# A scheduling priority around two groups of stages in a one-layer trunk kernel

## The chip, the core and the metric

The kernel runs on one core of a Trainium2 chip. The core has five engines with a queue each: PE (TensorE, matmuls), DVE (VectorE), ACT (ScalarE), POOL (GpSimd) and SP (SyncE, which here issues DMAs only). Each engine takes its instructions in the order of the program and waits at one whose inputs are not there. The metric is the device time of one execution in microseconds; times of kernels are medians of several runs.

## What is computed

One layer over 512 tokens with 1024 features, all in float32:

```python
h = rms_norm(x, g_mix)
p = h @ w_in
y_a = mla_group(p[..., :MLA_COLS], ...)     # 8 heads of latent attention, block-causal
y_b = rwkv7_group(p[..., MLA_COLS:], ...)   # 8 heads of a delta-rule recurrence over the tokens
x = x + concat(y_a, y_b) @ w_o
x = x + peer_ffn(rms_norm(x, g_ffn), ...)   # below
...
q = (hb @ w_pq).reshape(TOK_BLOCK, PEER_HEADS, 2, PEER_DHALF)
s = einsum('thpd,hpnd->thpn', q, sub_keys)
s1, i1 = top_k(s[:, :, 0], 16); s2, i2 = top_k(s[:, :, 1], 16)
top_s, pos = top_k(s1[..., :, None] + s2[..., None, :], 16)     # of 256 sums
idx = take_along_axis(i1 * 128 + i2, pos)                       # 16 of 16384 experts, per head
act = gelu(einsum('thkd,td->thk', expert_u[idx], hb))
out = einsum('thk,thkd->td', softmax(top_s) * act, expert_v[idx])
```

Each of the 16384 experts has one row of 1024 numbers in `expert_u` and one in `expert_v`, 64 MB each.

## The kernel before

The tokens are four blocks of 128. Every block runs through five stages, each a Python generator: F (`front`: norm and the projection for the recurrence), R (`chunks`: the recurrence's chunk-local products, with an inverse of triangular systems that alternates PE, line 674, and DVE, line 683), M (`latent`: the attention), S (`scan`: the recurrence over chunks) and B (`back`: output projection, line 792; retrieval, whose queries are line 848 on PE and whose top-16 lists are lines 827 to 835 on DVE; and routing, which ends on PE in line 947 and then writes the indices `idx` on ACT, line 960). I write F0 for stage F of block 0 and so on; blocks 1 and 2 share one B stage, B12. Block 0 and block 3 each have a B of their own, B0 and B3, the latter being the last entry of the list `BACK`.

Then the experts are worked off in two ways. Blocks 1 and 2 are dense: `dense()` goes through all experts in 128 tiles, with `up(e)` (line 1103 or 1117 on PE), `gate_half` (lines 1035 to 1043) and `down(e)` (line 1134 on DVE, then 1138 or 1149 on PE). Blocks 0 and 3 gather: `experts(b)` fetches, for each of 128 places (8 heads x 16), one row of `expert_u` per token by an indirect DMA that POOL issues (line 978), multiplies and sums it on DVE (line 988), and later does the same with `expert_v` (line 991). That makes 256 gathered tiles of 512 KB per block, 512 in all, in a ring of four buffers `ga`. One gather row below means one of these tiles and its DVE instruction.

A loop emits the steps of the stages in an order worked out from rough costs (`at`), `dense()` and the two `experts` behind them all. This is not yet the order on the engines. A scheduler goes over all the emitted instructions and fills each engine's queue with whatever it holds to be ready, by the priority of an instruction, lowest number first. The priority is a counter that rises by one with each instruction that is emitted. Waits are added where an instruction needs another engine's result or a buffer that is still in use. All loads of weights and tokens go through SP's queue in its order.

Of the kernel before, what the change touches and what calls it, by code (L numbers as in the profile page):

```python
# [29 lines left out]
TOPK = 16  # L30
# [5 lines left out]
# columns of the packed per-channel vectors  # L36
# [7 lines left out]
# columns of the packed per-feature rows  # L44
# [6 lines left out]
# candidate pairs (a, b) of the two sorted lists that can be among the best 16 sums, in order of a * 16 + b:  # L51
# (a, b) has (a + 1) * (b + 1) - 1 pairs before it that are at least as large
# [3 lines left out]
# lanes of stages: buffers, banks and weight tiles (count, width) of each  # L56
# [7 lines left out]
# blocks whose tokens gather their experts' rows, blocks that go through all experts  # L64
GATHERED = (0, 3)
DENSE = (1, 2)
EARLY = 1
GROUP, GA = 32, 4
# dense blocks: gates of HALF * 128 experts at a time, in GBUFS tiles of SUB * 128; activations run AHEAD tiles ahead,
# FIRST of them before the first gates, KEPT more wait in DRAM  # L70
HALF, SUB, GBUFS = 64, 16, 5
# [5 lines left out]
def u_whole(e):  # L77
    """float32 products of four passes, where the vector engine has no time to split; else three exact parts"""
    return e < 28 or 47 <= e - AHEAD < 64
# [7 lines left out]
def layer_kernel(ctx: ExitStack, tc: tile.TileContext, x, pos, cvec, rvec, w_mla, w_rwkv, w_uq, w_ukv, lora, g2,  # L87
# [5 lines left out]
    # what the last block's tail needs lies apart: its pools outlive those of the other stages  # L93
# [4 lines left out]
    # the tail takes over the buffers of the second lane  # L98
# [41 lines left out]
    # ---------------------------------------------------------------- constants  # L140
# [65 lines left out]
    # rows (beta s | kappa s), columns (alpha t | rho t)  # L206
# [52 lines left out]
    # rotary tables, token-major  # L259
# [50 lines left out]
    def square_sum(src, scr, acc):  # L310
        """the squares go to a tile that is written after them"""
        act(scr, src, AF.Square, accum_out=acc)

    def head_squares(src, n, acc, h0=0):
        """acc[:, h0 + i] = sum of squares of src[:, i, :n]"""
# [3 lines left out]
    # ---------------------------------------------------------------- stages  # L319
    def norm_in(xt, hT, carry):  # L320
        """channel-major normalized tokens, after the last one of the block before"""
# [19 lines left out]
    def rwkv_in(b, hT):  # L341
        pm = {}
        if b == EARLY:
            # the gather's buffers are idle until the first block's experts are known
# [16 lines left out]
    def mla(b, hT, yT):  # L361
# [31 lines left out]
        # queries  # L393
# [32 lines left out]
        # keys and values  # L426
# [27 lines left out]
        # block-causal attention, four heads at a time  # L454
# [73 lines left out]
    def rwkv_chunks(b, pm):  # L528
# [68 lines left out]
        # bonus weight and gate  # L597
# [8 lines left out]
        # values, token-major  # L606
# [680 lines left out]
```

## Time and profile before

| what | value |
|---|---|
| time, median of 3 runs | 1789.7 us (1786.15 to 1790.7) |
| profiled execution, first to last instruction (span) | 1781.3 us |
| mean granted TensorE clock in it | 0.950 of full speed |
| instructions | 29137 |
| DMA | 520.71 MB, 292 GB/s on average |

The profiled execution is one of its own; its span counts from the first to the last instruction and leaves out what lies around it, which is why it is shorter than the times of the runs. In the rows further down, an engine's busy time comes with a count of instructions; the idle time in front of a group stands in square brackets, with the name of what ended it; PEld is PE's weight loads; the granted clock is the share of TensorE's full speed.

### The profile page before, as it was taken

The page shows a single profiled execution, that of the slowest core. Times are in us where ns is not written, and L with a number is a line of the kernel's source. Part 1 is how long each engine was busy: PE and PEld are TensorE (multiplying, and loading weights), DVE is VectorE, ACT ScalarE, POOL GpSimd, SP SyncE. Part 2 cuts the span into 40 slices and gives each one's busy share as a digit, 9 for nine tenths or more (in the row PEclk, how much of TensorE's full clock was granted, in tenths as well). Part 3 has the DMA queues.
Part 4 walks back from the last instruction along what each step waited for, and adds up shares of the span by engine and source line. Part 5 has one row for each costly group of instructions (what it writes and reads, how often), then busy time and mean ns, then how long its engine had stood idle before and what let it go on. Part 6 is the DMA issues. An engine that isn't in the chain of part 4 may idle for free. (4 is left out here: it accounts for less than half of the span.)

```text
span 1781.3 us, 29137 instructions
## 1 busy us (share of the span) xinstructions
PE 1651.5 (93%) x10183; PEld 1394.3 (78%) x10183; DVE 1334.4 (75%) x2987; ACT 932.6 (52%) x2465; POOL 702.6 (39%) x562
## 2 busy tenths in 40 slices
PE   7999999998999998788997899999999999999987
PEld 6897799787867987567995577888777778888864
DVE  3412414775586789887789789998887799999898
ACT  5656454644545332367774334444768645445443
POOL 1001100244554444454443253334455446356453
PEclk9998999997697999988999999999989999999999
DMA  7634565596689988789997799998989999999988
GB/s 272 196 122 135 164 233 194 203 337 223 213 309 329 324 321 294 290 283 310 364 331 250 258 359 352 359 355 325 327 312 319 312 343 351 366 318 371 346 293 330
DMA packets 154866, 520.71 MB, mean 292 GB/s; under 512 B 17312, under 2 KB 24096, under 8 KB 154720
## 3 DMA queue, kind: packets, MB, share of 16 engines
q0 software_dynamic: 73728, 268.47, 43.1%
q1 hardware_dynamic: 80992, 250.39, 39.6%
q8 instruction: 80, 1.31, 0.3%
q14 instruction: 66, 0.54, 0.1%
HBM read 508.96 MB, written 9.83 MB: 291 GB/s over the span
## 5 line engine op out<-in xcount | busy, mean ns | idle before, releaser
L978 POOL DMA_INDIRECT ga<-in_expert_v_dram,idx x256 | 352.3, 1376 | 381.7 <-DVE acc L991 285.5
L978 POOL DMA_INDIRECT ga<-in_expert_u_dram,idx x256 | 299.8, 1171 | 372.0 <-DVE ga L988 257.5
L991 DVE SCALAR_TENSOR_TENSOR acc<-ga,dots,acc 128x1024 f32<-128x1024 f32 x256 | 327.9, 1281 | 65.9 <-DMA ga<-in_expert_v_dram,idx 64.9
L988 DVE SCALAR_TENSOR_TENSOR ga<-ga,h 128x1024 f32<-128x1024 f32 x256 | 311.6, 1220 | 52.3 <-DMA ga<-in_expert_u_dram,idx 52.1
L1149 PE MATMUL po<-xh,t 128*128 128x512 f32 x880 | 307.7, 407 | 12.7 <-DVE t L1064 5.7
L1117 PE MATMUL ps<-dh,ul 128*128 128x256 f32 x664 | 191.1, 288 | 7.9 <-DVE ul L1064 7.4
L1149 PEld LDWEIGHTS po<-xh,t 128*128 128x128 f32 x880 | 159.6, 192 | 48.6 <-ACT xh L1063 13.2
L1117 PE MATMUL ps<-dh,uh 128*128 128x256 f32 x664 | 189.8, 286 | 6.5 <-ACT uh L1063 6.5
L1149 PE MATMUL po<-xl,t 128*128 128x512 f32 x440 | 179.6, 408 | 14.6 <-DVE xl L1064 14.2
L1117 PE MATMUL ps<-dl,uh 128*128 128x256 f32 x664 | 187.5, 282 | 0.0
L1063 ACT ACTIVATE xh<-v 128x512 fp32r<-128x512 f32 x220 | 134.6, 626 | 96.4 <-PE po L1149 73.9
L1103 PE MATMUL ps<-t,u 128*128 128x256 f32 x720 | 172.6, 393 | 9.1 <-DMA u<-in_expert_ut_dram 8.8
L1103 PEld LDWEIGHTS ps<-t,u 128*128 128x128 f32 x720 | 138.5, 197 | 32.3 <-issue 6.3
L1064 DVE TENSOR_TENSOR xl<-v,xh 128x512 fp32r<-128x512 f32 x220 | 147.7, 690 | 16.2 <-ACT xh L1063 15.7
L1043 PEld LDWEIGHTS ps<-B,A 128*128 128x128 f32 x1024 | 131.3, 204 | 35.3 <-ACT ge L951 10.6
L1039 ACT ACTIVATE A<-iotap,slots 128x128 f32<-128x128 f32 x512 | 156.1, 395 | 0.0
L1043 PE MATMUL ps<-B,A 128*128 128x64 f32 x1024 | 131.5, 285 | 23.6 <-DVE B L1036 10.4
L1063 ACT ACTIVATE uh<-u 128x512 fp32r<-128x512 f32 x166 | 98.5, 625 | 83.8 <-PE ps L1117 52.0
L1117 PEld LDWEIGHTS ps<-dh,ul 128*128 128x128 f32 x664 | 126.4, 190 | 17.3 <-DVE ul L1064 13.4
L1117 PEld LDWEIGHTS ps<-dh,uh 128*128 128x128 f32 x664 | 126.4, 190 | 17.1 <-ACT uh L1063 10.0
L1117 PEld LDWEIGHTS ps<-dl,uh 128*128 128x128 f32 x664 | 126.4, 190 | 3.5 <-issue 0.7
L848 PE MATMUL ps<-h2T,wst 128*128 128x128 f32 (+1 forms) x768 | 125.1, 318 | 3.1 <-DMA wst<-in_w_pq_dram 3.1
(402 smaller groups left out, 2924.1 us busy)
## 6 DMA issues: line engine op xcount, KB each, us to landing
u<-in_expert_ut_dram SPq DMA_DIRECT2D x128, 512.0 KB, 6.7
v<-in_expert_v_dram SPq DMA_DIRECT2D x128, 512.0 KB, 6.6
wst<-in_w_rwkv_dram SPq DMA_DIRECT2D x56, 512.0 KB, 4.4
wst<-in_w_pq_dram SPq DMA_DIRECT2D x48, 512.0 KB, 6.7
wst<-in_w_o_dram SPq DMA_DIRECT2D x24, 512.0 KB, 5.2
wst<-in_w_mla_dram SPq DMA_DIRECT2D x16, 336.0 KB, 3.9
t<-in_x_dram SPq DMA_DIRECT2D x8, 512.0 KB, 4.6
wst<-in_w_ukv_dram SPq DMA_DIRECT2D x16, 256.0 KB, 3.5
```

The lines of the kernel that those rows point to most:

```text
L848: mm(p[:, :nb * P], w[:, kc, :], h2T[:, kc, :], start=kc == 0, stop=kc == KC - 1)
L978: G.indirect_dma_start(out=t, out_offset=None, in_=table, in_offset=bass.IndirectOffsetOnAxis(ap=idx[:, j:j + 1], axis=0))
L988: V.scalar_tensor_tensor(u, u, 1.0, h2, op0=OP.mult, op1=OP.mult, accum_out=dots[:, j:j + 1])
L991: V.scalar_tensor_tensor(acc, row_of(expert_v, j), dots[:, j:j + 1], acc, op0=OP.mult, op1=OP.add)
L1039: act(A[:, j, :], iotap, AF.Abs, scale=-1.0, bias=i2T[:, t0 + j:t0 + j + 1])
L1043: mm(p[:, j * HALF:(j + 1) * HALF], A[:, j, :], B[:, j, :], start=True, stop=True)
L1063: act(hi, t, AF.Copy)
L1064: V.tensor_tensor(lo, t, hi, op=OP.subtract)
L1103: mm(p, u[:, kc, :], hd[kc // 2][:, kc % 2, :], start=kc == 0, stop=kc == KC - 1)
L1117: mm(p, a[:, k, :], h[:, kc, :], start=kc + i == 0, stop=kc == KC - 1 and i == 2)
L1149: mm(po[i][n], ww[:, i * P:(i + 1) * P], vv, start=e + k == 0, stop=e == P - 1 and k == 2)
```

## The change

Each step of a stage of block 0, and each step of B3, is run within a guard that takes 4000 off the priority counter for the instructions emitted in it:

```diff
+URGENT = 4000
...
         lane[0] = LANE[n]
         try:
-            next(running[i])
+
+            with tc.high_priority(offset=URGENT) if bs == (0,) or (n, bs) == BACK[-1] else nullcontext():
+                next(running[i])
             at[i] += cost / count
         except StopIteration:
             for b in bs:
```

The other lines of the diff import `nullcontext` and empty the comments. No instruction that works on data is added or taken away: the engines' rows are the same, tile by tile, in another order.

How the counter moves can be read while the kernel is built. When a step returns, the guard puts the counter back. When a stage ends, its `StopIteration` passes through the guard, and the counter stays 4000 down. So its value on entering a step is -3886 in all of F0, -7885 in R0 and M0 (the last steps of R0 -11877), -15876 in S0, -15865 and rising in F1, -19672 and rising in B0, about -18900 and rising in the stages of blocks 2 and 3 that follow B0, -20520 in B3, and -20514 where `dense()` and `experts` begin. The constants, which are emitted first, have numbers above zero.

The order of the instructions on three engines, before and after; a tile's name ends in its number, and line numbers of the changed file are one higher there.

SP's queue (all DMAs of weights and tokens) at its very start, before; `t_84` are block 0's tokens, `t_1317` those of block 1, `cv` and `posi` small constants:

```order
L143 DMA t_84<-in_x_dram 128x1024
L149 DMA cv<-in_cvec_dram 128x67
L261 DMA posi<-in_pos_dram 128x4
L294 DMA wst_279<-in_w_rwkv_dram 128x1024
L294 DMA wst_292<-in_w_rwkv_dram 128x1024
L294 DMA wst_306<-in_w_rwkv_dram 128x1024
L162 DMA rv<-in_rvec_dram 128x192
L294 DMA wst_465<-in_lora_dram 128x512
L294 DMA wst_482<-in_w_mla_dram 128x672
```

The start of the same queue in the changed kernel:

```order
L295 DMA wst_1309<-in_g_dram 128x512
L295 DMA wst_482<-in_w_mla_dram 128x672
L295 DMA wst_465<-in_lora_dram 128x512
L295 DMA q_490<-in_w_mla_dram 128x672
L295 DMA k_494<-in_w_mla_dram 128x672
L295 DMA wst_486<-in_w_mla_dram 128x672
L163 DMA rv<-in_rvec_dram 128x192
L295 DMA wst_279<-in_w_rwkv_dram 128x1024
L295 DMA wst_292<-in_w_rwkv_dram 128x1024
L295 DMA wst_306<-in_w_rwkv_dram 128x1024
L144 DMA t_84<-in_x_dram 128x1024
L144 DMA t_1317<-in_x_dram 128x1024
```

Block 0's tokens went from the first place to the eleventh, behind ten loads of weights and one row of constants among them.

PE's queue near the end of B0, before; line 947 is B0's routing, 748 a product of S1, 399 the query projection of M2, 568 the beginning of R2:

```order
L947 MATMUL ps_2775<-t_2738,identb 128x128
L748 MATMUL ps_3291<-t_2204,t_2512 128x128
...
L389 MATMUL ps_3074<-ident,t_3053 128x128 x2
...
L399 MATMUL ps_3102<-wst_3104,t_3065 128x384
...
L568 MATMUL ps_3494<-bdm,t_3367 128x2 x2
```

The same place in the changed kernel; line 487 (486 before) are attention scores of M2, 691 and 693 the inverse of R2, 498 transposed probabilities of M2:

```order
L487 MATMUL ps_3842<-t_3834,t_3808 128x128
L691 MATMUL ps_3974<-t_3959,YB 128x64 x8
...
L948 MATMUL ps_2775<-t_2738,identb 128x128
...
L693 MATMUL ps_3975<-Y_160,TB 128x64 x3
...
L498 MATMUL ps_3869<-ident,t_3848 128x128
...
L675 MATMUL ps_4024<-t_3992,INT 128x64 x2
```

The attention and the inverse of block 2 now stand between the routing products of block 0, where only their beginnings stood.

DVE's queue around R3's last step of the inverse that DVE takes part in (`t_5615`, line 683), before; `ga` and `acc` are gather rows, `tv` and `ti` the top-16 lists of B12:

```order
L988 SCALAR_TENSOR_TENSOR ga_15158,dots_14835<-ga_15158,h_14833 128x1024
L991 SCALAR_TENSOR_TENSOR acc_14831<-ga_15161,dots_14835,acc_14831 128x1024
L827 MAX tv_4984<-t_5281 128x8 x4
L683 TENSOR_TENSOR t_5615<-ps_5606,lm_145 128x512
L988 SCALAR_TENSOR_TENSOR ga_15164,dots_14835<-ga_15164,h_14833 128x1024
L829 MAX_INDEX ti_4986<-tv_4984,t_5281 128x8
```

And in the changed kernel:

```order
L989 SCALAR_TENSOR_TENSOR ga_15140,dots_14835<-ga_15140,h_14833 128x1024
L992 SCALAR_TENSOR_TENSOR acc_14831<-ga_15143,dots_14835,acc_14831 128x1024
L989 SCALAR_TENSOR_TENSOR ga_15146,dots_14835<-ga_15146,h_14833 128x1024
L828 MAX tv_4984<-t_5437 128x8 x4
...
L832 MATCH_REPLACE t_5437<-tv_4984,t_5437 128x128
L684 TENSOR_TENSOR t_5615<-ps_5606,lm_145 128x512
L992 SCALAR_TENSOR_TENSOR acc_14831<-ga_15149,dots_14835,acc_14831 128x1024
```

R3's row now stands behind the top-16 work on B12's list `t_5281`, and in the work on the list after it (`t_5437`), but five gather rows further forward in the gather.

## Rows read from the trace of the kernel before

**Rows 1.** Part 1 of the page: busy us, share of the span, instructions.

```profile
PE 1651.5 (93%) x10183; PEld 1394.3 (78%) x10183; DVE 1334.4 (75%) x2987; ACT 932.6 (52%) x2465; POOL 702.6 (39%) x562
```

**Rows 2.** Busy time of each engine by stretch of the span.

```profile
core 0: us, PE busy (x) PEld busy (x) DVE busy (x) ACT busy (x) POOL busy (x), PEclk, DMA share, GB/s
0.00:338.00 338.00, 321.15 (x2426) 276.74 (x2427) 122.92 (x541) 189.75 (x603) 26.26 (x32) 0.98 0.57 185
338.00:421.00 83.00, 80.55 (x638) 69.24 (x637) 56.25 (x118) 43.19 (x144) 41.22 (x35) 1.00 0.88 310
421.00:476.00 55.00, 51.61 (x240) 48.15 (x241) 29.96 (x49) 27.61 (x69) 23.48 (x19) 0.50 0.58 189
476.00:640.00 164.00, 159.05 (x906) 127.16 (x906) 117.79 (x246) 75.03 (x222) 84.48 (x75) 0.91 0.92 317
640.00:953.00 313.00, 275.35 (x1698) 240.71 (x1697) 270.74 (x863) 180.52 (x487) 140.62 (x120) 0.93 0.89 312
953.00:1782.00 829.00, 763.76 (x4280) 632.29 (x4280) 736.79 (x1175) 416.49 (x943) 386.52 (x283) 0.98 0.91 329
```

**Rows 3.** Instructions on idx: ns min/median/max, then start of the first and last, us.

```profile
L978 POOL DMA_INDIRECT ga<-in_expert_u_dram,idx x256: 933/1086/3800, 338.7 to 1676.2; - x128
L978 POOL DMA_INDIRECT ga<-in_expert_v_dram,idx x256: 932/1152/6302, 433.9 to 1766.6; - x128
L960 ACT ACTIVATE idx<-ps x2: 268/272/277, 338.2 to 995.7; 128x128 int32<-128x128 f32 x2
```

**Rows 4.** Gather issues (line 978) by stretch.

```profile
core 0: us, POOL busy (x), PEclk, DMA share, GB/s
640.00:953.00 313.00, 136.29 (x117) 0.93 0.89 312
1250.00:1440.00 190.00, 100.31 (x80) 0.95 0.89 313
```

**Rows 5.** What DVE waited for, 338 to 640 us.

```profile
DVE ga L988 <- DMA ga<-in_expert_u_dram,idx: 27.4, 19, 4.2
...
DVE acc L991 <- DMA ga<-in_expert_v_dram,idx: 16.7, 12, 3.5
```

**Rows 6.** What DVE waited for, 640 to 953 us.

```profile
DVE acc L991 <- DMA ga<-in_expert_v_dram,idx: 18.9, 13, 3.0
DVE ga L988 <- DMA ga<-in_expert_u_dram,idx: 10.7, 10, 2.4
```

**Rows 7.** DMA issues from 0 to 20 us: count, KB each, us to landing.

```profile
wst<-in_w_rwkv_dram SPq DMA_DIRECT2D x4, 512.0 KB, 5.2
t<-in_x_dram SPq DMA_DIRECT2D x3, 512.0 KB, 6.0
wst<-in_w_mla_dram SPq DMA_DIRECT2D x4, 336.0 KB, 6.3
q<-in_w_mla_dram SPq DMA_DIRECT2D x1, 336.0 KB, 9.2
k<-in_w_mla_dram SPq DMA_DIRECT2D x1, 336.0 KB, 8.7
wst<-in_lora_dram SPq DMA_DIRECT2D x1, 256.0 KB, 8.3
wst<-in_g_dram SPq DMA_DIRECT2D x1, 256.0 KB, 8.0
rv<-in_rvec_dram SPq DMA_DIRECT2D x1, 96.0 KB, 7.4
```

**Rows 8.** ACT in order of time, from the start: start, length, us.

```profile
4.52 1.06 ACT L312 ACTIVATE hT<-t 128x1024 f32<-128x1024 f32 x1 [2.50 <-DMA t<-in_x_dram]
...
17.55 1.06 ACT L312 ACTIVATE hT<-t 128x1024 f32<-128x1024 f32 x1 [0.58 <-DMA t<-in_x_dram]
```

**Rows 9.** PE in order of time, its first work on tokens.

```profile
10.78 1.97 PE L333 MATMUL ps<-ident,t 128*128 128x128 f32 x8 [6.97 <-ACT t L325]
```

**Rows 10.** PE in order of time, the last products of R3's inverse before line 683.

```profile
631.22 0.33 PE L674 MATMUL ps<-t,INT 128*128 128x64 f32 x2
```

**Rows 11.** DVE in order of time, at R3's last line 683, and at the first `down`.

```profile
634.58 1.28 DVE L991 SCALAR_TENSOR_TENSOR acc<-ga,dots,acc 128x1024 f32<-128x1024 f32 x1 [3.52 <-DMA ga<-in_expert_v_dram,idx]
...
636.56 0.67 DVE L683 TENSOR_TENSOR t<-ps,lm 128x512 f32<-128x512 f32 x1
...
952.98 1.61 DVE L1134 TENSOR_TENSOR q<-q,G 128x256 f32<-128x256 f32 x3
```

More of the change, by code (lines that the diff above doesn't have):

```diff
@@ L1 @@
 import math
-from contextlib import ExitStack
+from contextlib import ExitStack, nullcontext
 import concourse.bass as bass
```

## The prediction

> **What bounds the kernel now.** I began with the page: PE is busy 93% of the span and DVE 75% [rows 1]. One engine's share says little here, so I cut the span where the code changes its work [rows 2]. Up to 338 us PE is busy 321 of 338 us and DVE 123: the front is PE work, and after PE's start at 10.8 us [rows 9] it is idle for only 6 us there. From 640 to 953 us DVE is busy 271 of 313 us, and from 953 us to the end 737 of 829, while PE is idle for 38 us and 65 us: the back half is an in-order DVE queue in which gather rows (`experts`) alternate with rows of `gate_half`, `down` and the routing. The gather is the third party. Its first issue is at 338.7 us, right behind block 0's `idx` (338.2), its last at 1766.6 us [rows 3], 15 us before the end, so it spans four fifths of the time. From 640 to 953 us it took 2.68 us a row (117 issues), from 1250 to 1440 us, the stretch in which it ran freest, 2.38 (80 issues) [rows 4]. DVE waited 44.1 us for gathered rows from 338 to 640 us [rows 5] and 29.6 from 640 to 953 [rows 6], so the gather is often late there. In the program's order, 108 of the 512 gather rows stand ahead of R3's last L683 row on DVE, and 226 ahead of the first row of `down` (L1134).
>
> **What the change does to the order.** It does not bring block 0 forward. The guard takes 4000 off the counter, and a stage that ends leaves it there, so code that is emitted later outranks code emitted earlier; the constants and F0 rank lowest of all, and R0 and M0 next. The rows of the order show it in three places, and each is a term.
>
> *The start.* The load of block 0's tokens (`t_84`) was SP's first DMA and is now its eleventh. Ahead of it stand 256 + 336 + 256 + 3 x 336 + 96 + 3 x 512 = 3488 KB [rows 7]. Before, its 512 KB had landed by 4.52 us, and the token load of F1, with which 4548 KB had been asked for, by 17.55 us, where ACT waited for it [rows 8]. That is 310 KB per us between the two, and so 4000 KB by 15.8 us: **11.3 us later**. PE's first transposes, 6.3 us behind the landing [rows 8, 9], move to 22 us. What is loaded ahead is needed anyway, so a little may come back; I take nothing off, since PE has hardly any idle time afterwards.
>
> *Block 0's routing.* I gave each PE row of the new order its busy time in this trace and summed. Ahead of B0's last L947 row stood 320.6 us of PE work; now it is 372.4. The 51.8 us more are 22.4 of M2, 20.2 of R2, 6.0 of S1, 2.5 of S2 and 0.7 of F3, part of the 132 us that PE did from 338 to 476 us [rows 2]. 7.5 of them ran where the granted clock was 0.50 (421 to 476 us), 1.2 of 2.4 GHz, and would take half at full clock. So the first gather goes from 338.7 to 338.7 + 11.3 + 51.8 - 3.7 = **398 us**.
>
> *The inverse of block 3 (R3).* Ahead of its last L674 products on PE stood 603.9 us of work, now 648.7: 19.6 of the dense blocks' first `up` tiles (40 matmul rows of L1103, none before), 16.0 of B12's queries and 9.3 of M3. They began at 631.2 us [rows 10]; with 11.3 + 44.9 that is 687 us. Against this stands the clock. From 421 to 476 us PE did 51.6 us of work at 0.50, small products of R2 and M2; now these lie mixed with F3's 128x129 products. Nothing comes back, or 26 us; I take 13, since the stretch behind it was slow in part too (0.91 over 476 to 640 us). PE: 674 us. The gather must have brought 103 rows by then: 398 + 103 x 2.38 to 2.68 = 643 to 674 us, so it may bind as well, as before, when DVE waited 3.52 us for a gather just ahead of this row [rows 11]. I set DVE's L683 row at **675 us, 38 later** than 636.6; the ends are 662 and 692.
>
> *From there to the first `down`.* Before, this took 316 us (636.6 to 953.0), of which DVE worked 274.0. In the new order 258.4 us of DVE work lie between the same two rows: 7.1 more stand ahead of R3's row and 8.4 less ahead of `down`, where 219 gather rows stand in place of 226. With the 42 us of idle time kept this takes 301 us; by the gather, 116 rows at 2.38 to 2.68 take 276 to 311. I take the middle of the latter, 294: first `down` at **969 us, 16 later**. So 22 of the 38 us are given back here, at the price of PE idle time.
>
> *From `down` to the end* the two orders run alike, with the gather 3 to 7 rows behind its old place; 744.4 us of DVE work remain in place of 736.0. At the ratio of before, 829 us for 737, that is **9 us**, seen as gather rows behind the last `xx` rows. B3's `idx` is no limit: it is ready at 996 us [rows 3], when some of block 0's rows are still to come (30 of 256 behind the first `down`), and B3's PE work is not moved against it.
>
> Sum: 16 + 9 = 25 us on a span of 1781.3, so 1806 us. The median of the three runs, 1789.7, lies 8.4 above this span; the same distance gives 1815 us.
>
> **A rule weighed.** PE shows 321 busy us of 338 at the start, its weight loads 277 [rows 2]. The Trainium skill, "Perfetto Trace Analysis", section "Identifying the Most-Contended Engine", says that matmul busy time is a poor measure of how full TensorE is and that LDWEIGHTS busy time should be read instead. By it PE had 61 us to spare up to 338 us, the delays of 11 and 52 us could be made up within that, and the sum would be near zero. No row of this trace shows TensorE taking more work in that time, which leaves it a rival's case (the third).
>
> **The rivals.**
> 1. *The gather alone counts (longer).* All 512 rows keep the mean pace of before, (1766.6 - 338.7) / 511 = 2.79 us, from 398 us on: the end moves by the whole 59 us, to 1849. For it: the gather runs to the last. Against it: it did 2.38 where DVE let it, and in the new order its rows outrank the rest. Chance 0.15.
> 2. *The clock comes back (faster).* The stretch from 421 to 476 us runs at full clock (26 us), so does what was slow up to 640 us (half of 2 x 0.09 x 164, some 15 us), R3's handoff falls at 660 us, and the gather rows, first in rank, wait less: 275 us to the first `down`, at 935. Then 935 - 953 + 9 = -9 us, 1781. It decides where `down` begins before 939 us. For it: from 421 to 476 us PE ran 240 matmul records in 55 us at 0.50, against 638 in the 83 us before at 1.00 [rows 2]. Against it: the 45 us of PE work moved ahead of R3. The Trainium skill, "TensorE: Matmul & The Clock Gate", Part 1, says that sustained activity is what releases the full clock; the two stretches agree. Chance 0.13.
> 3. *Nothing to see.* PE's queue has more room than its busy time tells, or DVE's 42 us of idle time cover the rest: the handoff falls near 660, `down` at 939 to 949, and the time stays within 0.3%. Chance 0.12.
>
> **How the numbers follow.** The forecast, a loss of 6 to 50 us, has 0.60. A measurement of this kernel can tell about 0.3%, 5.4 us. Slower by more: 0.60 + 0.15 = 0.75; within: 0.12; faster: 0.13. The range adds the ends: 662 to 692 at R3 (-13, +17) and 276 to 311 behind it (-18, +17) around +25 give -6 to +59: 1783 to 1850 us. Left out are most of rival 2 and a tail above.
>
> **What would show it.** In the trace of the changed kernel: PE's first transposes near 22 us; the first gather issue near 398 us; a granted clock well over 0.50 between 400 and 480 us; R3's last inverse row on DVE near 675 us; the first `down` near 969 us; gather rows alone behind the last `xx`. I would be wrong if the first gather came before 380 us, if R3's row came before 655 us, or if DVE, between that row and the first `down`, lost its waits for gathered rows or doubled them.

## The result, and the profile after

The changed kernel takes **1839.9 us** (median of 4 runs, 1830.9 to 1854.1) against 1787.9 for the kernel before on the same chips: a ratio of 1.032, 95% interval 1.026 to 1.038, some 52 us where 25 were forecast. The direction was right and the time lies in the range; the size was half. The profiled execution spans 1829.0 us (before 1781.3). All ratios, here and in the experiments, and e8's times leave out the few runs over 1.5% above the fastest of the same kernel (one of ten in e2, e8 and e10, two of ten in e4, at 1815 and 1823 us).

First part 1 of the page of the changed kernel, then its busy time by stretch, which answer to [rows 1, 2] (line numbers of the changed kernel are one higher than before):

```profile
PE 1641.4 (90%) x10183; PEld 1385.7 (76%) x10183; DVE 1336.6 (73%) x2987; ACT 932.0 (51%) x2461; POOL 704.5 (39%) x562
```

```profile
core 0: us, PE busy (x) PEld busy (x) DVE busy (x) ACT busy (x) POOL busy (x), PEclk, DMA share, GB/s
0.00:338.00 338.00, 304.63 (x2088) 258.78 (x2089) 85.81 (x288) 180.18 (x573) 24.28 (x31) 0.93 0.49 157
338.00:421.00 83.00, 80.41 (x671) 71.64 (x670) 57.61 (x293) 43.74 (x151) 7.49 (x6) 0.96 0.49 156
421.00:476.00 55.00, 55.00 (x472) 52.94 (x471) 31.69 (x72) 26.06 (x72) 23.74 (x23) 1.00 0.86 327
476.00:640.00 164.00, 146.56 (x870) 112.20 (x870) 109.94 (x196) 81.69 (x238) 84.12 (x70) 0.91 0.86 297
640.00:997.00 357.00, 291.97 (x1811) 257.33 (x1809) 305.98 (x956) 182.57 (x489) 166.11 (x143) 0.89 0.87 311
997.00:1829.00 832.00, 762.82 (x4280) 632.77 (x4280) 745.58 (x1185) 417.77 (x941) 398.77 (x290) 0.97 0.92 333
```

In the rows, the granted clock (PEclk) of 1.00 is 2.4 GHz and 0.50 is 1.2 GHz. Up to 338 us PE is 16.5 us less busy than before, at a mean granted clock of 0.93 in place of 0.98, with 2088 matmul records in place of 2426. The slow stretch from 421 to 476 us is gone (1.00 for 0.50). The last stretch, from the first `down` on, is as before: 832 us for 829. So nearly all of the loss is made ahead of `down`.

The instructions on `idx`, as in [rows 3] (shortest, median and longest in ns, then the start of the first and the last):

```profile
L979 POOL DMA_INDIRECT ga<-in_expert_u_dram,idx x256: 935/1026/3386, 427.6 to 1727.6; - x128
L979 POOL DMA_INDIRECT ga<-in_expert_v_dram,idx x256: 935/1152/3832, 514.1 to 1815.1; - x128
L961 ACT ACTIVATE idx<-ps x2: 267/272/278, 427.0 to 1039.3; 128x128 int32<-128x128 f32 x2
```

The first gather comes at 427.6 us, not at 398: 89 us later than before, not 59. ACT and PE in order of time at the start, as in [rows 8, 9]:

```profile
15.91 1.06 ACT L313 ACTIVATE hT<-t 128x1024 f32<-128x1024 f32 x1 [11.79 <-DMA t<-in_x_dram]
```

```profile
19.41 1.97 PE L334 MATMUL ps<-ident,t 128*128 128x128 f32 x8 [15.59 <-ACT t L326]
```

The tokens land at 15.9 us (15.8 forecast) and PE starts 8.6 us later than before. PE by line from 120 to 160 us, the changed kernel and then the kernel before (busy us, mean ns of one, idle time ahead):

```profile
L675 PE MATMUL ps<-t,INT 128*128 128x64 f32 x48 | 8.3, 340 | 0.0
L691 PE MATMUL ps<-t,YB 128*128 128x64 f32 x32 | 7.2, 418 | 0.9 <-DVE os L511 0.9
L693 PE MATMUL ps<-Y,TB 128*128 128x64 f32 x16 | 3.6, 421 | 0.0
L693 PE MATMUL ps<-t,TB 128*128 128x64 f32 x16 | 3.6, 421 | 0.0
...
L355 PE MATMUL ps<-hT,wst 128*128 128x129 f32 x16 | 2.1, 280 | 0.0
```

```profile
L354 PE MATMUL ps<-hT,wst 128*128 128x129 f32 x42 | 5.7, 280 | 0.0
...
L674 PE MATMUL ps<-t,INT 128*128 128x64 f32 x32 | 4.0, 273 | 0.0
L692 PE MATMUL ps<-t,TB 128*128 128x64 f32 x32 | 3.8, 273 | 0.0
...
L690 PE MATMUL ps<-t,YB 128*128 128x64 f32 x22 | 2.8, 270 | 0.0
```

Here R0's 128x64 products lie mostly by themselves, and the same product (line 690, now 691) takes 418 ns in place of 270. Before, F1's products (line 354) stood among them. The difference in duration goes with the granted clock, not with the neighbours: in the changed kernel 16 such products in a row took 2.00 us while the clock was at 1.00, and 3.52 us a little later at 0.50. Two rows of the windows for the clock, two of PE in order of time (start, length) for the products:

```profile
124.00:128.00 4.00, 3.48 (x27) 3.13 (x27) 0.99 (x4) 3.27 (x12) 0.00 (x0) 1.00 0.39 129
132.00:152.00 20.00, 18.76 (x88) 18.45 (x88) 1.94 (x6) 8.91 (x26) 1.65 (x1) 0.50 0.00 1
```

```profile
125.82 2.00 PE L675 MATMUL ps<-eye,INT 128*128 128x64 f32 x16
133.21 3.52 PE L691 MATMUL ps<-t,YB 128*128 128x64 f32 x16
```

One row of the windows, 100 to 260 us, sums it up, first for the kernel before, then for the changed one:

```profile
100.00:260.00 160.00, 157.02 (x1172) 133.97 (x1172) 39.72 (x100) 93.09 (x296) 10.96 (x10) 0.97 0.51 165
```

```profile
100.00:260.00 160.00, 151.46 (x1000) 127.72 (x999) 40.17 (x98) 84.30 (x279) 9.90 (x8) 0.86 0.35 108
```

PE did 172 matmul records fewer in that time, at 0.86 of full clock in place of 0.97. From the start up to the write of `idx`, the kernel before and then the changed one:

```profile
0.00:338.20 338.20, 321.35 (x2428) 276.94 (x2429) 122.92 (x541) 189.95 (x605) 26.26 (x32) 0.98 0.57 185
```

```profile
0.00:427.00 427.00, 391.04 (x2815) 336.14 (x2816) 147.31 (x595) 229.12 (x736) 31.77 (x37) 0.94 0.48 155
```

Last, what PE waited for from 700 to 997 us (us, times, longest), what DVE waited for from 640 to 997 us, as in [rows 6], and DVE in order of time at R3's last line 684 and at the first `down`, as in [rows 11]:

```profile
PE ps L912 <- DVE t L920: 29.3, 2, 17.8
PE ps L720 <- DVE ST L757: 12.5, 1, 12.5
PE ps L910 <- DVE t L926: 8.3, 9, 3.8
```

```profile
DVE acc L992 <- DMA ga<-in_expert_v_dram,idx: 26.4, 20, 3.5
DVE ga L989 <- DMA ga<-in_expert_u_dram,idx: 17.5, 17, 3.1
```

```profile
700.90 0.69 DVE L684 TENSOR_TENSOR t<-ps,lm 128x512 f32<-128x512 f32 x1
...
996.60 0.56 DVE L1135 TENSOR_TENSOR q<-q,G 128x256 f32<-128x256 f32 x1
```

PE waits 50 us for DVE's rows of the scan and the routing (in the kernel before, from 700 to 953 us, 2.2 us). DVE itself waited 43.9 us for gathered rows (before 29.6, in 313 us).

### The profile page after: what moved, and what is told of

It reads as the page before. It is cut to its first block, busy times and chain, and to the rows that moved or that the text cites. A ratio compares the mean times of both kernels' runs of the same rounds, so it can differ in the third digit from the quotient of the medians.

```text
span 1829.0 us, 29195 instructions
## 1 busy us (share of the span) xinstructions
PE 1641.4 (90%) x10183; PEld 1385.7 (76%) x10183; DVE 1336.6 (73%) x2987; ACT 932.0 (51%) x2461; POOL 704.5 (39%) x562
## 4 chain that ended last, share of the span: by engine, by line
PE 48%; DMA 19%; DVE 13%; issue 10%; POOL 5%; ACT 4%; SPq 0%; POOLq 0%; DVEq 0%; ACTq 0%
DMA ga<-in_expert_v_dram,idx 10%; PE po L1150 9%; PE ps L1118 8%; PE ps L355 5%; POOL ga L979 5%; PE ps L849 4%; DMA ga<-in_expert_u_dram,idx 4%; DVE ga L989 3%; DVE acc L992 3%; DMA v<-in_expert_v_dram 2%; PE ps L675 2%; PE po L1139 2%; PE ps L1044 2%; PE ps L1104 2%; PE ps L691 1%
## 5 line engine op out<-in xcount | busy, mean ns | idle before, releaser
L979 POOL DMA_INDIRECT ga<-in_expert_u_dram,idx x256 | 304.1, 1188 | 367.8 <-DVE ga L989 218.0
L1150 PE MATMUL po<-xl,t 128*128 128x512 f32 x440 | 178.4, 406 | 11.3 <-DVE xl L1065 11.0
L1044 PEld LDWEIGHTS ps<-B,A 128*128 128x128 f32 x1024 | 127.4, 200 | 17.0 <-ACT A L1041 8.6
L1044 PE MATMUL ps<-B,A 128*128 128x64 f32 x1024 | 127.4, 281 | 6.8 <-ACT A L1041 6.5
```

Of the source, the lines that this page charges most:

```text
L979: G.indirect_dma_start(out=t, out_offset=None, in_=table, in_offset=bass.IndirectOffsetOnAxis(ap=idx[:, j:j + 1], axis=0))
L1044: mm(p[:, j * HALF:(j + 1) * HALF], A[:, j, :], B[:, j, :], start=True, stop=True)
L1150: mm(po[i][n], ww[:, i * P:(i + 1) * P], vv, start=e + k == 0, stop=e == P - 1 and k == 2)
```

## The experiments

Some numbers go with each run. *Ahead* is the PE work that stands ahead of block 0's routing in its order, by the durations of before, as the prediction worked it out. *First row* is the start of DVE's first gathered row (line 988), *lost* the difference of the two in whole us: the time up to there in which PE did not advance at its old pace (start, waits, low clock). *Rows* is the gather rows ahead of the first `down`.

| run | ahead | first row | lost | rows | first `down` | ratio to before, 95% |
|---|---|---|---|---|---|---|
| before | 321 | 344.4 | 23 | 226 | 953.0 | 1 |
| changed | 372 | 433.0 | 61 | 219 | 996.6 | 1.032 (1.026 to 1.038) |
| e1 | 372 | 434.6 | 63 | 208 | 975.8 | 1.028 (1.021 to 1.035) |
| e2 | 321 | 347.5 | 27 | 224 | 946.9 | 1.004 (1.000 to 1.007) |
| e3 | 321 | 352.5 | 32 | 224 | 959.5 | 1.007 (1.005 to 1.010) |
| e4 | 371 | 398.5 | 28 | 203 | 938.5 | 1.004 (1.001 to 1.008) |
| e5 | 352 | 414.5 | 63 | 217 | 986.8 | 1.019 (1.012 to 1.027) |
| e6 | 330 | 363.6 | 34 | 230 | 959.4 | 1.006 (1.002 to 1.009) |
| e9 | 374 | 445.8 | 72 | 224 | 1021.5 | 1.034 (1.026 to 1.043) |
| e10 | 320 | 340.8 | 21 | 248 | 973.7 | 1.008 (1.004 to 1.012) |
| e11 | 321 | 349.0 | 28 | 228 | 952.5 | 1.003 (0.999 to 1.007) |
| e12 | 330 | 393.6 | 64 | 231 | 1006.9 | 1.030 (1.023 to 1.036) |
| e13 | 334 | 371.5 | 38 | 226 | 962.4 | 1.014 (1.005 to 1.023) |
| e14 | 317 | 349.6 | 33 | 234 | 963.9 | 1.009 (1.005 to 1.013) |
| e15 | 319 | 365.2 | 46 | 225 | 969.2 | 1.019 (1.012 to 1.027) |
| e16 | 358 | 400.1 | 42 | 210 | 962.8 | 1.021 (1.014 to 1.028) |
| e17 | 336 | 395.9 | 60 | 228 | 991.2 | 1.016 (1.012 to 1.021) |
| e18 | 358 | 383.6 | 26 | 215 | 938.0 | 1.001 (0.997 to 1.004) |

**One half of the edit at a time (e1, e2).**

```diff
 with tc.high_priority(offset=URGENT) if bs == (0,) else nullcontext():             # e1
 with tc.high_priority(offset=URGENT) if (n, bs) == BACK[-1] else nullcontext():    # e2
```

> The guard is put around the stages of block 0 alone; block 3's output projection runs without it, so the dense blocks and the experts, emitted last, are no longer lifted a second time. PE's order up to block 0's routing is that of the changed kernel (372 us of work ahead of it by the durations of before), the last inverse products of R3 stand behind 631 us of PE work (before 629, changed 684), and 87 gather rows stand ahead of R3's last row on DVE (before 108, changed 103). Theory 1, the late start of the gather is the loss: first gathered row used near 433 us, as in the changed kernel (433.0), R3's row anywhere up to 700, and the end still 35 to 60 us later than before, 1825 to 1850 us. Rival 2, the PE work put ahead of R3 is the loss: R3's row on DVE comes 20 to 45 us earlier than in the changed kernel, at 656 to 680 us, and most of the loss goes with it: 1790 to 1815 us. Rival 3, it is the second lift of the dense blocks and the experts: the time is that of before within 6 us.

> The guard is put around block 3's output projection, retrieval and routing alone. The front is as before (321 us of PE work ahead of block 0's routing, x0's load first on SP), and what is emitted after that stage, the dense blocks and the experts, stays lifted by 4000. Gather rows ahead of R3's last row on DVE 104 (before 108), ahead of the first down 224 (226). Theory 1, late start of the gather: it starts at 344 us as before, and the time is that of before within 8 us, 1780 to 1796. Rival 3, the lift of the dense blocks and the experts is the loss: 1815 to 1840 us with an unaltered front.

The loss is block 0's half (+54 us); the second lift of what is emitted last costs at most some tenths of a per cent. In e1 R3's row came at 662.0 us (changed 700.9), as rival 2 said, but the loss did not go with it.

**The start, and the late routing, each by itself (e3, e4).**

```diff
-    x0 = load_x(0)
+    with tc.high_priority(offset=-200):                                            # e3
+        x0 = load_x(0)
```

```diff
+URGENT = -600                                                                      # e4
+            with tc.high_priority(offset=URGENT) if (n, bs) == ("B", (0,)) else nullcontext():
+                ended = next(running[i], True)
+            if ended:
+                raise StopIteration
```

> The kernel before, with one line edited: the load of block 0's tokens ranks 200 lower, which makes it SP's eleventh DMA, as in the changed kernel. PE's order in the front is that of before (321 us ahead of block 0's routing). It measures the first term of the sum, the start, by itself. Theory 1: PE's first transposes come 8 to 11 us later (near 19.4 us, as in the changed kernel), the first gather 8 to 11 us later, near 353 us, and the end 4 to 9 us later, 1792 to 1797 us. Rival, PE makes the start up within its idle time: the first gather within 3 us of 344 and the time within 4 us of before.

> The kernel before, with block 0's output projection, retrieval and routing ranked 600 lower while they run (the rank is given back when the stage ends), and nothing else. 371 us of PE work stand ahead of block 0's routing in place of 321 (changed: 372), the start and the stages F0, R0, M0 and S0 are as before, and R3's last inverse products stand behind 610 us of PE work in place of 629. Gather rows ahead of R3's last row on DVE 72 (before 108), ahead of the first down 203 (226). Theory 1, the late start of the gather is the loss: first gathered row used near 394 us (+50), and though R3 comes earlier the end is 20 to 35 us later, 1808 to 1825 us. Rival 2, PE's work ahead of R3 decides: R3's row comes some 20 us earlier, and the time is 0 to 20 us shorter than before, 1768 to 1790 us.

In e3 the load came sixth, not eleventh as the expectation has it, and PE's first transposes only 2.7 us later; it is a weak test of the start, which e14 makes properly. e4 is the run that broke theory 1. The gather began 54 us later, about as far as PE's order was moved:

```profile
L979 POOL DMA_INDIRECT ga<-in_expert_u_dram,idx x256: 935/1084/4701, 392.9 to 1706.1; - x128
```

and the time rose by 8 to 9 us, not by 20 to 35. Nor did it fall, as rival 2 allows, though R3's row came 43 us earlier (594.0). Work that PE does in another order is not lost: block 0's routing waits, other stages come earlier, and 23 gather rows fewer stand ahead of `down`.

**The start mended, and the guard closed (e5, e6).** e5 is the changed kernel with the first two loads lifted; e6 is the change with the rank given back when a stage ends.

```diff
+    with tc.high_priority(offset=40000):                                           # e5
+        x0 = load_x(0)
         ...
+        nc.sync.dma_start(cv, cvec)
```

```diff
-                next(running[i])
+                ended = next(running[i], True)                                     # e6
+            if ended:
+                raise StopIteration
```

> The changed kernel, with the loads of block 0's tokens and of the packed vectors lifted by 40000, so that x0 is SP's first DMA again. 352 us of PE work (durations of before) stand ahead of block 0's routing (before 321, changed 372), and R0's last products still stand behind 163 us (before 128, changed 163); 102 gather rows ahead of R3's last row on DVE, 217 ahead of the first down. The first four runs left this theory: from the first gathered row to the first down the gather sets the pace at 2.6 to 2.7 us a row, whatever the order, so down begins at the first row's time plus rows ahead times that pace, and each row left for later costs 1.2 to 1.6 us behind it. By it: first gathered row near 404 us (29 earlier than in the changed kernel: 9 of start, 20 of PE work), down at 404 + 217 x 2.6 = 968, the end near 1801, a time of 1800 to 1820 us. If instead the low clock and the waits of the front hang on R0's products lying alone, which this kernel does not mend, the first gathered row comes only at 415 to 425 and the time is 1815 to 1835.

> The change as its words say it: the guard is around the same stages, and the rank is given back when a stage ends, so nothing that is emitted later is lifted. x0 is still SP's eleventh DMA. 330 us of PE work ahead of block 0's routing (before 321, changed 372), R0's last products behind 145 us (128; 163) among products of F1, R3's behind 629 as before; gather rows ahead of R3's last row on DVE 122 (108), ahead of the first down 230 (226). By the pace theory: first gathered row at 344 + 9 + 9 = 362 us, down at 362 + 230 x 2.65 = 971, the end 821 behind it less 5 for four rows fewer: +13 to +20, a time of 1793 to 1805 us. The rival, block 0 brought forward is a gain once the leak is shut: first gathered row at or before 344 us and a time under 1780.

e5 gave back about a third: its time, 1818.6 us, lies in the spans of both theories, but its first row came at 414.5 us, as late as the second theory has it, with a granted clock of 0.83 from 100 to 260 us. e6 loses 0.6%, less than forecast (1788.4 us against 1793 to 1805): the guard as such is nearly free, and what it leaks makes the loss. It is no gain either: block 0's routing comes later in it, not earlier.

**Without block 0's gather (e7, e8).** e7 is the kernel before and e8 the changed one, each without block 0's 256 gather rows and with block 0's output left unfinished; they serve for their times alone.

```diff
+        if b == 0:
+            nc.sync.dma_start(out[b * P:(b + 1) * P, :], acc)
+            return
```

> The kernel before without block 0's experts: its 256 gathered rows and their work on DVE are left out, and block 0's output is its input to the experts. Nothing is gathered until block 3's indices are ready. It is the base of the next run. PE is left as the bound of the first 950 us; its work is 1649 us in the kernel before, so the time is some 1660 to 1720 us, and R3's last row on DVE comes at 620 to 660 us.

> The changed kernel without block 0's experts, as the run before. Order on PE: R3's last products behind 692 us of work against 655 in the run before, block 0's routing behind 372 against 317, B12 behind 746 against 715, B3 behind 860 against 846. If the loss of the change is TensorE's (work put ahead of R3, low clock and waits in the front), it is there without the gather too: R3's row 50 to 75 us later than in the run before, and a time 30 to 50 us longer. If it is the gather's (late first row, then a fixed pace), most of it is gone: R3's row still later by 40 or more, but the time within 15 us of the run before.

1730.2 us (1727.6 to 1733.4) and 1770.2 us (1754.7 to 1779.9): the change costs 40 us, 2.3%, where no row is gathered until block 3's routing. R3's row moved by 50 us (664.0 to 713.5). So the gather need not carry the loss. PE up to 430 us in e7 and then in e8:

```profile
0.00:430.00 430.00, 410.92 (x3045) 353.47 (x3046) 151.89 (x609) 233.12 (x750) 32.47 (x37) 0.96 0.54 171
```

```profile
0.00:430.00 430.00, 392.11 (x2788) 335.85 (x2789) 146.09 (x591) 226.81 (x729) 31.76 (x37) 0.93 0.48 153
```

18.8 us less busy and at a lower clock: PE is behind by the front, with or without a gather.

**The place of block 3's stages (e9, e10, e11).** A second guard, given back, lifts F3, R3 and S3 in the changed kernel (e9) and in the kernel before (e10); in e11 R3 alone ranks lower.

```diff
+    with tc.high_priority(offset=20000) if bs == (3,) and n in "FRS" else nullcontext():   # e9, inside the change's guard
+    with tc.high_priority(offset=4000) if bs == (3,) and n in "FRS" else nullcontext():    # e10
+    with tc.high_priority(offset=-700) if (n, bs) == ("R", (3,)) else nullcontext():       # e11
```

> The changed kernel with the stages F3, R3 and S3 lifted by 20000 while they run (that lift is given back). The front is that of the changed kernel (372 us of PE work ahead of block 0's routing, first gathered row near 433 us, 224 rows ahead of the first down), but R3's last products stand behind 577 us of PE work in place of 684, S3's behind 629 in place of 709. Three theories are left. The place of R3 and S3: the routing of block 3 and with it the first down wait for them; put early, they give the loss back, first down at or before 965 us, time 1780 to 1805. The gather's pace: first down at 433 + 224 x 2.6 = 1015, time 1830 to 1850, wherever R3 stands. TensorE's lost time alone (start, waits and low clock in the front, some 20 us net up to 700 us): that stays, the waits behind 700 us go, first down near 970 to 980, time 1800 to 1820.

> The kernel before, with the stages F3, R3 and S3 lifted by 4000 while they run, the rank given back at their end: R3's last products behind 562 us of PE work (before 629), S3's behind 617 (690), the rest of PE's order within 5 us of before, 106 gather rows ahead of R3's last row on DVE and 248 ahead of the first down (226). The place of R3 and S3: what is late costs, so what is early gains, first down 10 to 25 us earlier, time 1760 to 1775. The gather's pace: first down at 344 + 248 x 2.65 = 1001, less 1.4 us for each of 22 rows fewer behind it, 1795 to 1805. TensorE's lost time alone: the work ahead of down is the same and PE has 32 us of idle time from 700 to 953 us, so within 10 us of before.

> The kernel before, with the stage R3 alone ranked 700 lower while it runs: R3's last products behind 655 us of PE work (before 629, changed 684), S3's behind 709 (690; 709). The front up to F3 is that of before, with 228 gather rows ahead of the first down (226). The place of R3 and S3: R3's row on DVE 20 to 30 us later, first down 12 to 20 later, time 1793 to 1803. The gather's pace and TensorE's lost time: within 6 us of before.

R3's row on DVE came at 637.0 us in e9 (changed 700.9) and the kernel lost no less, 3.4%; at 597.6 in e10, which lost 0.8%; at 685.0 in e11, 48 later than before, with no loss that can be told. The place of R3 decides nothing. In all three the first `down` stands where the gather's pace puts it, 2.55 to 2.65 us a row behind the first row.

**R0 early in the changed kernel (e12).**

```diff
+    with tc.high_priority(offset=20000) if (n, bs) == ("R", (0,)) else nullcontext():      # inside the change's guard
```

> The changed kernel with the stage R0 lifted by 20000 while it runs, so that its small products come early: R0's last behind 126 us of PE work (before 128, changed 163), block 0's routing behind 330 (321; 372), R3's last behind 567 (629; 684). x0 stays SP's eleventh DMA. It mends the front but not the start. TensorE's lost time: up to 430 us PE is at full clock and idle no more than 10 us beyond the start, and the time is 1785 to 1800. If the loss were in what is emitted late (M3, the dense blocks) it would stay near 1830.

It did not mend the front: R0 came early (155.9 us), M0 in its place late (its last product at 191 us against 149). The work ahead of the routing is near that of before, the lost time is 64 us, and the loss stays, where 1785 to 1800 us were forecast for the case that TensorE's lost time decides. This is the counterpart of e4: order nearly restored, time lost, 3%.

**What loses the time: the leak behind the front, the start, R0's place (e13 to e16).** e13 and e14 have the change's guard, leak and all, around other stages; e15 has no leak; e16 is the changed kernel with F1 ranked lower.

```diff
+    ... if (n, bs) == ("B", (0,)) or (n, bs) == BACK[-1] else nullcontext():        # e13
+    ... if bs == (0,) and n in "F" or (n, bs) == BACK[-1] else nullcontext():       # e14
+    with tc.high_priority(offset=-1000) if (n, bs) == ("R", (0,)) ...               # e15, given back
+    with tc.high_priority(offset=-8000) if (n, bs) == ("F", (1,)) ...               # e16, given back, inside the change's guard
```

> The guard of the change, but around block 0's output projection (its last stage) and block 3's alone, and as in the change not given back at their ends. The front is as before (x0 first on SP, R0's last product behind 128 us of PE work, 334 us ahead of block 0's routing, before 321); behind it the order is much like that of the twelfth run (M3 behind 663 us, R3 behind 555, S3 behind 658, 226 gather rows ahead of the first down). Lost time in the front, that is the first gathered row's time less the PE work ahead of block 0's routing, is 23 us in the kernel before and 61 in the changed one. If that is the cause: 23 to 30 here, the first gathered row at 357 to 364 us, the time within 10 us of before. If the cause is what the leak lifts behind block 0: the time is 1820 or more, as in the twelfth run.

> The guard of the change around block 0's first stage F0 and block 3's output projection alone, not given back at their ends. x0's load is SP's eleventh DMA as in the changed kernel, R0's last product stands behind 133 us of PE work among F1's (before 128, changed 163), 317 us stand ahead of block 0's routing (321; 372). It has the late start and not R0's place. The lost time of the front: 23 us before, 8 to 9 more for the start, 30 to 36 here; the first gathered row at 347 to 353 us, the time 5 to 14 us over before. If the start is the main cause, the lost time is 50 or more and the time 25 us or more over before.

> The kernel before with R0, block 0's inverse, ranked 1000 lower while it runs, the rank given back: no leak, x0 first on SP. On PE R0's last product stands behind 163 us of work and F1's behind 96, just as in the changed kernel (before 128 and 123), block 0's routing behind 319 (before 321). So R0's small products lie without F1's among them, and that is nearly all that differs. If this is where the front loses its time: PE's granted clock falls below 0.85 somewhere from 100 to 260 us and its idle time grows, the lost time rises from 23 to 40 us or more, first gathered row at 360 us or later, time 15 to 40 us over before. If not: lost time under 30, time within 6 us of before.

> The changed kernel with F1's stage ranked 8000 lower while it runs, which puts its products back among R0's: F1's last behind 141 us of PE work (before 123, changed 96), R0's behind 147 (128; 163), block 0's routing behind 358 (321; 372), 210 gather rows ahead of the first down (226; 219). The late start (x0 eleventh) and the rest of the leak stay. If R0's place is where the front loses its time: the lost time falls from 61 us to 30 to 42, first gathered row at 388 to 400, the time 5 to 20 us over before, though block 0's routing is still 37 us of work later. If the leak acts behind the front: 1825 or more.

e14: the start costs 9 us of lost time and 16 us in all. e15: R0's place by itself costs 23 us of lost time and 29 us in all; its row from 100 to 260 us:

```profile
100.00:260.00 160.00, 153.78 (x1044) 128.18 (x1042) 41.10 (x101) 92.09 (x294) 10.98 (x10) 0.89 0.41 128
```

e13 and e16 lie between their two cases (+22 and +38 us, 10 and 20 forecast at most). In e16 the lost time fell as forecast, to 42 us, and the time did not follow. In e13 the lost time itself was missed: 38 us, where 23 to 30 were forecast, with the start and R0's place as before. So something of the leak is left in both.

**Both sources, without the leak and with it (e17, e18).**

```diff
+    with tc.high_priority(offset=-400):                                             # e17: and e15's edit
+        x0 = load_x(0)
```

e18 is e16 with e5's edit.

> The kernel before with two ranks changed and no leak: the load of block 0's tokens ranks 400 lower, which makes it SP's eleventh DMA as in the changed kernel, and R0 ranks 1000 lower while it runs. On PE R0's last product stands behind 164 us of work and F1's behind 96 (before 128 and 123, changed 163 and 96), block 0's routing behind 336 (321; 372); R3's behind 636, B12's 753, 228 gather rows ahead of the first down (629, 752, 226). If TensorE's lost time in the front is the cause and these two are its sources: lost time 50 to 60 us (before 23, changed 61), first gathered row at 386 to 396 us, the time 30 to 50 us over before. If the rest of the leak is needed for that: no more than the 29 us over before of R0's place alone.

> The changed kernel, leak and all, with the two sources mended: x0's and the packed vectors' loads lifted by 40000 (SP's first DMA again), and F1's stage ranked 8000 lower, which puts its products among R0's (F1's last behind 137 us of PE work, R0's behind 151). Block 0's routing stands behind 358 us (before 321, changed 372), R3 behind 646, 215 gather rows ahead of the first down. If the two are the cause: lost time 28 to 38 us, first gathered row at 386 to 396 us, the time 5 to 20 us over before. If the rest of the leak costs by itself: 30 us or more over before.

e18 settles the main point: with the leak in place, block 0's routing still behind 358 us of work and R3 behind 646 (before 321 and 629), but both sources mended, the time is that of before; 5 to 20 us over were forecast. Its start is a little better than mended: PE's first transposes come at 7.6 us, before at 10.8. Its row from 100 to 260 us, and its routing:

```profile
100.00:260.00 160.00, 159.19 (x1162) 136.02 (x1162) 40.23 (x101) 92.94 (x291) 11.41 (x10) 0.96 0.44 144
```

```profile
L962 ACT ACTIVATE idx<-ps x2: 258/268/278, 377.5 to 975.7; 128x128 int32<-128x128 f32 x2
```

e17 has the lost time of the changed kernel (60 us) and little over half of its loss (29 us, just under the span). Its waits of PE from 700 to 950 us are not those of the changed kernel:

```profile
PE ps L1045 <- DVE B L1038: 10.3, 1, 10.3
PE ps L911 <- DVE t L927: 5.5, 3, 2.5
```

No run points to a version that beats both kernels.

## Why the prediction was right in sign and half in size

**The step that failed is block 0's routing.** The prediction put 51.8 us for the order, 11.3 for the start and -3.7 for the clock: first gather at 398 us. Measured, 427.6. The order was right (372.4 us of work stand ahead); mis-sized was the rest, taken as 7.6 us of lost time. It is 37 us (60.6 less 23.8, to a tenth), and the two rows up to `idx` divide it. PE is idle for 36.0 us in place of 16.9: 8.6 of that are the later start, 10.5 are other waits. And it is busy for 391.0 us with work that took 372.4 in the trace of before: 18 us longer, when the 0.8 us is taken off by which that sum falls short for the kernel before too (320.6 of 321.4). For these waits and this slower work there was no term. e14 and e15 show the two sources each by itself (9 us of lost time from the start, 23 from R0's place), e17 both (37). The working gave each product the duration that it had in the trace of before. But those durations belonged to an order in which R0's products lay among F1's; in the new order they run at a granted clock of 0.50 for part of the way (132 to 152 us, 418 ns for 270) and wait for ACT and DVE. The clock's term had the wrong sign: the stretch from 421 to 476 us came back, as counted, and the front lost more.

**And its two parts were priced the wrong way round.** The 52 us of order were carried to the end as lateness of the gather. e4 and e18 have 50 and 37 us of such order, and lose 8 to 9 us and nothing. The lost time costs: the nine runs with gather and at least 38 us of it (the changed kernel among them) lose 1.4 to 3.4%, the eight with less lose 0 to 0.9%. e12 has the lost time and hardly the order, and loses 3%.

*The start*: 11.3 us forecast, 8.6 measured. *R3*: 675 forecast, 700.9 measured. The row is where the gather's bound puts it from its real start (433 + 103 x 2.6 = 701), so this miss is the first one carried on; but e9 to e11 show that this row was not the thing to watch. The signs of being wrong that the prediction named stayed out: it watched for a first gather that comes too early, not one that comes too late. *From there to `down`*: 294 forecast, 296 measured (996.6 - 700.9). *From `down` to the end*: 9 forecast, 5 measured (821.7 us before and 826.9 now from the first `down` to the last gathered row), with gather rows alone behind the last `xx`, as forecast. With 701 us for R3's row the prediction's own steps give 701 + 294 = 995 for `down` and 42 + 9 = 51 us on the span, which grew by 47.7: in the numbers the one term carried the whole error. That is no proof of the steps behind it: in e4 the first row came 54 us later and R3's row 43 us earlier, and the kernel lost 8 to 9 us; e8 lost 40 us without these rows. That the later terms fit so well is in part luck.

**The rivals.** *The gather alone* came nearest in its number (1849) and is wrong in its mechanism: e4 moves the gather's start by 54 us for 0.4%, and e8 loses 40 us with no gather of block 0. *The clock comes back*: it did from 421 to 476 us, and went elsewhere, in the front. The sentence of the Trainium skill that stood with it ("TensorE: Matmul & The Clock Gate", Part 1) is not borne out by busy time as these rows count it: PE was 94% busy in the slow stretch of before (51.61 of 55 us [rows 2]) and in that of the changed kernel (18.76 of 20 us), both at 0.50. That the two stretches of before agree with it, as the prediction says, is not shown. *Nothing to see*: PE had no hidden room. In e14 the start alone was not made up: 9 us of lost time, 16 us in all. The Trainium skill's rule on LDWEIGHTS ("Perfetto Trace Analysis", "Identifying the Most-Contended Engine"), by which 61 us were to spare in the front, does not foretell this kernel's time.

**What stays open.** Lost time sorts the runs, but it does not size them. At nearly the same lost time, 60 to 64 us, the runs lose 29 (e17), 39 (e5) and 52 to 56 us (e1, e12, changed). PE's 50 us of waits for DVE's scan and routing rows in the changed kernel do not explain this: e17 has them not, but neither has e1, which loses as much as the changed kernel. From 700 to 976 us it has on such rows only

```profile
PE ps L910 <- DVE t L926: 10.2, 11, 4.2
```

Nor do the parts add up: e16 and e18 differ in the edit of the first two loads alone, and it gives back all of e16's 38 us, while e14 prices the late start at 16. And e13 loses some 14 us more than before in the front with neither source in it. What else the leak costs was not tried by itself.

The rival that comes closest is the gather's pace. If the delay of the first row counts in full, and each row less ahead of `down` is worth 2.6 us there and costs 1.3 us behind it (an estimate from the pace of these runs and from DVE's 1.28 us a row [rows 11]), the runs come out in much the same order, but the sizes are wrong where order was moved: 80 us for the changed kernel, 24 for e4 and 25 for e18, which lose 52, 8 to 9 and none. And e8 loses 40 us without block 0's rows. A share of the loss by this way, once the rows start late, is not excluded.

Why the granted clock falls where R0's products lie alone is not shown either; that it does, and comes back when F1's lie among them, is (0.86 in the changed kernel and 0.89 in e15 from 100 to 260 us, against 0.97 before and 0.96 in e18).

## What to carry to other kernels

When a change reorders an engine that is already full, ask first whether work is lost or only moved: work that trades places costs little, time in which the engine stands or runs slowly comes out at the end, here at four fifths of its length or more. Do not price a new order with the old order's durations: look which small, dependent products lose the large, independent ones that stood among them, and take their time from a stretch in which they ran alone. And a guard around a generator's step must be left also on the step that ends it, or it changes the rank of all that follows.

## What the runs showed that was not expected

- PE can look full and run at half clock: from 132 to 152 us of the changed kernel it was busy for 18.76 of 20 us at a granted clock of 0.50, and 16 products of 128x64 in float32 took 3.52 us there, 2.00 a few us before at 1.00.
- Leaving out half of all gathered rows shortens the kernel by only 2.8% (interval 2.2 to 3.5%), though the gather runs for four fifths of the span: block 0's gather is not what bounds the kernel.
- From the first gathered row to the first `down`, all orders with block 0's gather need 2.55 to 2.71 us a row, whether the rows start at 341 or 446 us. This pace foretold the times of e9 and e10 and still is not the cause of the loss.
- Runs of the kernel before lie between 1768 and 1797 us over the chips used, so a difference of 0.3 to 0.5% is at the edge of what a run here tells.
